# Linear attention's norm and gate as a stream of their own, and sample values that no longer wait for the mix

## The chip, the cores and the metric

The kernel runs on one core of a Trainium2 chip. The metric is the time of one execution on the device in microseconds. The kernel before took 2499.03 us (median of three runs, 2498.38 to 2510.2).

## The reference, cut to what matters

One layer of a hybrid decoder is computed for 1024 prompt tokens and for 32 sample tokens (8 sequences of 4), in fp32. After a first feed-forward network, one projection gives the columns of four mixers; their outputs go through `w_out`, and a second feed-forward network follows. Two mixers matter here.

The first is linear attention with a decaying state:

```
qe, ke, kd = q * exp(b), k * exp(-b), k * exp(b_last - b)      # b: running sum of the log decay in a chunk
att   = tril(qe @ ke.T);  o = att @ v + qe @ S                 # S: state of 32 x 64 per head, 4 heads
S     = exp(b_last) * S + kd.T @ v                             # from chunk to chunk
o     = o * rsqrt(mean(o * o) + EPS)  * norm_g * silu(g)       # per head: the norm and the gate
```

Prompt chunks have 64 tokens. The sample tokens are eight chunks of 4, each with a state of its own that is read from memory, and whose new state is an output.

The other is dilated attention: three groups of four heads with windows of 128, 512 and 2048 at dilations of 1, 4 and 16. The outputs of the three groups are merged with weights from their softmax denominators. The sample tokens attend to cached keys and values, 36 loads of 256 KB for the values alone.

## The kernel before, in words

**The mainline and the streams.** The large products form one sequence, `line()`, the mainline. Beside it run streams: Python generators that each issue a few instructions and yield. A recording layer, `Loom` (L1399), decides at build time in which order all of this is written down: it keeps a planned time for each engine, lets the stream with the best priority go that is ready (`run`, L1574), and takes the next step of the mainline (`weft`, L1530) where none is ready or where PE would be short of dense work. A stream can yield a condition (a lambda); it is then held until the condition is true. The engines work off their queues in the recorded order. On the chip itself nothing is decided.

**The stage of the change.** It begins behind the RWKV mixer and holds linear attention (`gla`), dilated attention (`dil`) and the last parts of the mainline: the remaining projection columns (products named `pw`, L139, L142, L143) and then the first half of the output projection (products named `pz`, L2897, 432 of them). When the mainline has reached its end, only the streams are left. The stage after it begins with the second half of the output projection (L204), which reads the mixers' results from the tiles `xl`.

**Linear attention** works in five pieces: four of 256 prompt tokens, and the 32 sample tokens. It has two streams of equal priority `GP` = 0.9. `operands` (L2422) loads q, k, v and the decays of a piece (tiles gq, gk, gv, gmn), makes `qe`, `ke`, `kd`, turns v and kd (products into `pm`, L2468 and L2485) and appends the operands to `made`; it is at most two pieces ahead. `outputs` (L2490) takes a piece, loads its gate columns into `ggt`, computes `o` (tile go) by `chunks` (L2507: L2514 state increments, L2530 scores, L2539 scores by values, L2543 query by state) or for the last piece by `sample` (L2553), and then norms and gates it by `gate` (L2594). In `sample` the products are L2561 (scores), L2573 (by values), L2576 (query by state, on the tile gSF, which POOL clears and ACT fills) and L2589 (the state's increments, from the tile gex). In `gate`, ACT squares `o` (L2600), PE takes the mean (L2606), DVE computes the reciprocal root in three steps (`rsqrt_steps`, L1009) and spreads it (L2610, tile gsp), PE turns it (L2616), DVE multiplies (L2618), POOL applies the gate (L2619), and two transfers write `mixd`. A piece's products begin only when the piece before it is gated: all of it is one generator.

**Dilated attention** has six heads' halves, which `prep` (L1998) loads and turns (kv: the sample rows, L2033), and 24 blocks of `attend` (L2054): scores L2065, softmax on DVE and ACT, turned weights L2096 copied to the tile pT (L2100 on ACT, L2102 on DVE, a ring of four), products with values L2107. `merge` (L2145) merges the groups in eight steps: two loads `ot` per step, DVE L2197 to L2202 and POOL L2199, then PE turns the result (L2206) into the tiles `mix`, which exist from the 20th block on. `sample` (L2211) first scores the cached keys (L2229; the window of 128 with products L2271 and L2276), then waits until `mix` exists, then runs `dil_sample` (L2282): 36 loads of values into a ring of four tiles (cv), 72 products (L2347), and at the end the result is turned (L2358) and copied into `mix`. `join` splits `mix` into `xl` by thirds of the tokens.

**What follows.** `mixes01` loads linear attention's result (mx from `mixd`) and splits it into `xl`, three thirds with two loads each. The first weights of the next stage are cast on ACT (L111) and on POOL (L112). The results of L204 go through DVE, ACT and POOL into the norm of the next stage and come back to PE as L312.

Of the kernel before, what the change touches and what calls it, by code (L numbers as in the profile page):

```python
# [11 lines left out]
F32 = mybir.dt.float32  # L12
F32R = mybir.dt.float32r
AF = mybir.ActivationFunctionType
# [6 lines left out]
TP = 1024  # L21
# [1927 lines left out]
def dil(L, pool, wload, xs3):  # L1949
# [48 lines left out]
    def prep(g, p, H):  # L1998
# [32 lines left out]
        nc.tensor.transpose(q[:32, 256:384], qs, ident)  # L2031
        kv = ap.tile([32, 3, 128], F32, name="kv", tag="kv", bufs=1)
        nc.scalar.copy(kv.rearrange("t u x -> t (u x)"), q[:32, 0:384])  # L2033
# [177 lines left out]
    def sample():  # L2211
        yield from dil_sample_keys(L, ap, qd, qz, caches, sT, groups, ps)
        yield lambda: len(mix) > 0
        yield from dil_sample(L, ap, tab[:, 384:], qz, kts, vs, caches, sT, mix, ps)
        sampled.append(1)
# [66 lines left out]
def dil_sample(L, ap, bias, qz, kts, vs, caches, sT, mix, ps):  # L2282
# [50 lines left out]
    for b0 in range(0, 8, 2):  # L2333
# [6 lines left out]
        for xs in ((0,), (1, 2), (3, 4), (5, 6), (7, 8)):  # L2340
# [11 lines left out]
            for i in range(len(xs)):  # L2352
                fetch(j - len(xs) + i + NR)
            yield 0.0
    q = ps("pa")
    for p in range(2):
# [22 lines left out]
def gla(L, ap, cold, mixd):  # L2379
# [19 lines left out]
    nc.vector.memset(scans.rearrange("p (c t) -> p c t", t=4)[:, :, 0:1], 0.0)  # L2399
    rows = ap.tile([3, 128], F32, name="glarows", tag="ga")  # L2400
    L.dma(rows[0:1], I["gla_b_alpha"])
# [9 lines left out]
    pieces = ((0, 256), (256, 256), (512, 256), (768, 256), (TP, TS))  # L2411
    made, through = [], [0]

    def tile(tag, shape=(128, 256), bufs=1):
        return ap.tile(list(shape), F32, name="g" + tag, tag="g" + tag, bufs=bufs)
# [6 lines left out]
    def operands():  # L2422
# [4 lines left out]
        yield lambda: L.loom.got(GLA)  # L2427
        al = [ap.tile([16, TH], F32, name="gal", tag=g) for g in ("ggt", "go", "gv")]
        for t in range(NTH):
# [60 lines left out]
    def outputs():  # L2490
        for j, (a, w) in enumerate(pieces):
            cl, nch, nt, n = dims(a, w)
            yield lambda: len(made) > j
            qe, ke, kn, Vn, ends = made[j]
            gt = tile("gt", (128, 2, 256))[:, :, :w]
            for p in range(2):
                L.dma(gt[:, p], cold["gla_g%d" % p][:, a:a + w])
            yield 0.0
            o = tile("o", (128, 2, 256))[:, :, :w]
            if a < TP:  # L2500
                yield from chunks(j, o, *made[j])
            else:
                yield from sample(o, *made[j])
            yield from gate(a, w, o, gt)
            through[0] = j + 1

# [87 lines left out]
    def gate(a, w, o, gt):  # L2594
# [3 lines left out]
        st = ap.tile([128, 8], F32, name="gst", tag="gst")[:n, :m]  # L2598
        sqs = tile("aT", (128, 2, 256))[:, :, :w]
        nc.scalar.activation(sqs, o, AF.Square)  # L2600
        yield
        q = ps("pt")
        for p in range(2):
            for i in range(nt):
                j = (p * nt + i) * 2
                nc.tensor.matmul(q[:n, j:j + 2], sqs[:, p, i * n:(i + 1) * n], b2m, start=True, stop=True)  # L2606
        nc.vector.tensor_scalar(st, q[:n, :m], EPS, None, op0=OP.add)
        rn = yield from rsqrt_steps(L, ap, st, (n, m), "grs")
        sp = ap.tile([128, 8, 64], F32, name="gsp", tag="gaT")[:n, :m]
        nc.vector.tensor_copy(sp, rn.unsqueeze(2).to_broadcast([n, m, 64]))  # L2610
        yield
        q = ps("pt")
        for p in range(2):
            for i in range(nt):
                j = (p * nt + i) * 2
                nc.tensor.transpose(q[:, p * w + i * n:p * w + i * n + n], sp[:, j:j + 2].rearrange("p h c -> p (h c)"), ident[:n, :n])  # L2616
        for p in range(2):
# [5 lines left out]

    return operands(), outputs()

# [554 lines left out]
```

## Time and profile before

| | |
|---|---|
| time, median of three runs | 2499.03 us |
| the profiled execution | 2503.86 us |
| its span, first to last instruction | 2502.1 us |
| mean granted clock of PE | 0.972 |

The span is that of one profiled execution, so sums are made against 2503.86 us. In the profile, PE is TensorE's matmuls, PEld its weight loads, DVE VectorE, ACT ScalarE, POOL GpSimd and SP the queue that issues most loads. A row of a group reads: line, engine, operation, output and inputs by the program's names, sizes, count, then busy us and mean ns of one, then the idle time of the engine just before them and what ended it. An fp32 product that the program records once shows as two rows in the trace (two passes); a turn (transpose) shows as one.

### The profile page before, as it was taken

The page shows a single profiled execution, that of the slowest core. Times are in us where ns is not written, and L with a number is a line of the kernel's source. Part 1 is how long each engine was busy: PE and PEld are TensorE (multiplying, and loading weights), DVE is VectorE, ACT ScalarE, POOL GpSimd, SP SyncE. Part 2 cuts the span into 40 slices and gives each one's busy share as a digit, 9 for nine tenths or more (in the row PEclk, how much of TensorE's full clock was granted, in tenths as well). Part 3 has the DMA queues.
Part 4 walks back from the last instruction along what each step waited for, and adds up shares of the span by engine and source line. Part 5 has one row for each costly group of instructions (what it writes and reads, how often), then busy time and mean ns, then how long its engine had stood idle before and what let it go on. Part 6 is the DMA issues. An engine that isn't in the chain of part 4 may idle for free. (4 is left out here: it accounts for less than half of the span.)

```text
span 2502.1 us, 41009 instructions
## 1 busy us (share of the span) xinstructions
PE 2411.0 (96%) x15543; PEld 2207.7 (88%) x15543; DVE 1395.5 (56%) x3211; ACT 1013.6 (41%) x2175; POOL 1067.8 (43%) x902
## 2 busy tenths in 40 slices
PE   8999999999999999999999999968999999999997
PEld 8999999977789998898888899737989999997777
DVE  7645454367775056665632467437854444447767
ACT  5433333366554242323324344415533333336651
POOL 3655555567643233232111111114355555557664
PEclk9999999999999999999989889969999999999999
DMA  4322222323434333231226676444222222233334
GB/s 133 100 69 83 66 82 68 106 86 111 119 126 132 93 106 90 87 100 52 74 56 195 185 228 184 134 130 146 79 86 74 80 74 80 72 103 92 104 103 148
DMA packets 273612, 265.21 MB, mean 106 GB/s; under 512 B 36283, under 2 KB 247380, under 8 KB 273414
## 3 DMA queue, kind: packets, MB, share of 16 engines
q1 hardware_dynamic: 223810, 212.69, 28.9%
q10 hardware_dynamic: 49604, 49.90, 5.8%
q8 instruction: 122, 2.00, 0.3%
q14 instruction: 76, 0.62, 0.1%
HBM read 195.26 MB, written 67.16 MB: 105 GB/s over the span
## 5 line engine op out<-in xcount | busy, mean ns | idle before, releaser
L520 POOL TENSOR_TENSOR wlo<-wraw,whi 128x512 fp32r<-128x512 f32 x280 | 379.7, 1374 | 355.1 <-ACT whi L519 355.0
L549 PE MATMUL p<-xh,whi 128*128 128x352 f32 x1120 | 364.0, 325 | 5.4 <-DVE hid L475 3.6
L551 PE MATMUL p<-xh,wlo 128*128 128x352 f32 x1120 | 362.3, 323 | 0.0
L550 PE MATMUL p<-xl,whi 128*128 128x352 f32 x1120 | 361.2, 322 | 0.0
L519 ACT CAST whi<-wraw 128x512 fp32r<-128x512 f32 x280 | 166.5, 620 | 409.1 <-PE p L550 293.4
L112 POOL TENSOR_TENSOR wlo<-wraw,whi 128x1024 fp32r<-128x1024 f32 x61 | 146.0, 2396 | 391.8 <-ACT whi L111 343.6
L139 PE MATMUL pw<-xh,whi 128*128 128x352 f32 x888 | 308.1, 347 | 2.3 <-ACT stg L2782 1.5
L143 PE MATMUL pw<-xh,wlo 128*128 128x352 f32 x888 | 293.4, 330 | 0.0
L142 PE MATMUL pw<-xl,whi 128*128 128x352 f32 x888 | 293.1, 330 | 0.0
L549 PEld LDWEIGHTS p<-xh,whi 128*128 128x128 f32 x1120 | 211.4, 189 | 6.8 <-DVE hid L475 3.9
L550 PEld LDWEIGHTS p<-xl,whi 128*128 128x128 f32 x1120 | 211.5, 189 | 0.0
L551 PEld LDWEIGHTS p<-xh,wlo 128*128 128x128 f32 x1120 | 210.4, 188 | 0.0
L139 PEld LDWEIGHTS pw<-xh,whi 128*128 128x128 f32 x888 | 171.5, 193 | 13.3 <-issue 7.5
L142 PEld LDWEIGHTS pw<-xl,whi 128*128 128x128 f32 x888 | 172.1, 194 | 1.9 <-issue 1.7
L143 PEld LDWEIGHTS pw<-xh,wlo 128*128 128x128 f32 x888 | 171.2, 193 | 1.4 <-issue 1.2
L549 PE MATMUL p<-hid,whi 128*128 128x352 f32 x400 | 129.9, 325 | 1.8 <-ACT n L583 1.4
L551 PE MATMUL p<-hid,wlo 128*128 128x352 f32 x400 | 129.8, 324 | 1.4 <-POOL wlo L520 1.4
L550 PE MATMUL p<-hid,whi 128*128 128x352 f32 x400 | 129.2, 323 | 0.0
L111 ACT CAST whi<-wraw 128x1024 fp32r<-128x1024 f32 x61 | 63.9, 1048 | 118.7 <-PE pw L142 85.2
L723 PE MATMUL p<-xh,hid 128*128 128x512 f32 x320 | 109.8, 397 | 0.1
L204 PE MATMUL pt<-whi,ya 128*128 128x256 f32 x512 | 97.7, 290 | 1.0 <-POOL ya L793 1.0
L839 DVE TENSOR_TENSOR y<-y,p 128x512 f32<-128x512 f32 x112 | 76.6, 685 | 38.7 <-PE p L723 36.7
(641 smaller groups left out, 5861.9 us busy)
## 6 DMA issues: line engine op xcount, KB each, us to landing
wraw<-in_w_ff_gate_dram SPq DMA_DIRECT2D x44, 512.0 KB
wraw<-in_w_ff_up_dram SPq DMA_DIRECT2D x44, 512.0 KB
wraw<-in_w_in_dram SPq DMA_DIRECT2D x37, 512.0 KB
wraw<-in_w_ff_down_dram SPq DMA_DIRECT2D x36, 512.0 KB
hid_d<-tmp ACTq DMA_DIRECT2D x60, 176.0 KB
hid_d<-n ACTq DMA_DIRECT2D x60, 176.0 KB
cv<-in_cache_win_dram SPq DMA_DIRECT2D x36, 256.0 KB
whi<-hid_d SPq DMA_DIRECT2D x32, 256.0 KB
```

What stands on the lines that cost most here:

```text
L112: nc.gpsimd.tensor_tensor(lo, raw, hi.bitcast(F32), op=OP.subtract)
L139: ins = nc.tensor.matmul(out, a, xh[:, cs], start=(first and i == 0), stop=False)
L142: nc.tensor.matmul(out, a, xl[:, cs], start=False, stop=False)
L143: nc.tensor.matmul(out, b, xh[:, cs], start=False, stop=(last and i == n - 1))
L204: nc.tensor.matmul(out, xs[kx][a][:, cs], ws[js[0]][b][:, kw], start=u == a == b == 0, stop=u == len(kk) - 1 and a == 1, skip_group_check= ...
L519: nc.scalar.copy(t[0][:, i], v)
L520: nc.gpsimd.tensor_tensor(t[1][:, i], v, t[0][:, i].bitcast(F32), op=OP.subtract)
L549: nc.tensor.matmul(out, ah, xh, start=first and k == 0, stop=False, skip_group_check=True)
L550: nc.tensor.matmul(out, ah, xl, start=False, stop=False, skip_group_check=True)
L551: nc.tensor.matmul(out, al, xh, start=False, stop=k == KH - 1, skip_group_check=True)
L723: nc.tensor.matmul(out, a[i][:, u], b[j][:, u], start=first and u == i == j == 0, stop=u == n - 1 and i == 1, skip_group_check=True)
L839: (nc.vector.tensor_copy if h else nc.scalar.copy)(v, p) if copy else nc.vector.tensor_add(v, v, p)
```

## The change

There are four parts. First, `gla` returns three streams: `gates` is new, between `operands` and `outputs`. `outputs` now only computes `o` and appends it to `raw`; `gates` loads the gate columns of a piece and norms and gates it, while `outputs` goes on with the next piece. For that `o` has two buffers (tag `go`). Second, the gate's squares and spreads are done in two halves of one tile `gsq`, in the place of the tiles gaT and gsp, which it shared with the scores. Third, the sample stream of dilated attention waits before its values for all six halves to be loaded and turned, and for `mix` only where it writes into it. Fourth, some tiles move: `kv` has no buffer of its own and takes one of the ring pT, and the first tiles of linear attention take other tags.

```diff
-        kv = ap.tile([32, 3, 128], F32, name="kv", tag="kv", bufs=1)
+        kv = ap.tile([32, 3, 128], F32, name="kv", tag="pT", bufs=4)
...
     def sample():
         yield from dil_sample_keys(L, ap, qd, qz, caches, sT, groups, ps)
-        yield lambda: len(mix) > 0
+        yield lambda: ready[0] == len(heads)
         yield from dil_sample(L, ap, tab[:, 384:], qz, kts, vs, caches, sT, mix, ps)
...
             yield 0.0
+    yield lambda: len(mix) > 0
     q = ps("pa")
     for p in range(2):
...
         for j, (a, w) in enumerate(pieces):
             cl, nch, nt, n = dims(a, w)
             yield lambda: len(made) > j
-            qe, ke, kn, Vn, ends = made[j]
+            o = tile("o", (128, 2, 256), 2)[:, :, :w]
+            if a < TP:
+                yield from chunks(j, o, *made[j])
+            else:
+                yield from sample(o, *made[j])
+            through[0] = j + 1
+            raw.append(o)
+
+    def gates():
+
+        for j, (a, w) in enumerate(pieces):
+            yield lambda: len(raw) > j
             gt = tile("gt", (128, 2, 256))[:, :, :w]
             for p in range(2):
                 L.dma(gt[:, p], cold["gla_g%d" % p][:, a:a + w])
             yield 0.0
-            o = tile("o", (128, 2, 256))[:, :, :w]
-            if a < TP:
-                yield from chunks(j, o, *made[j])
-            else:
-                yield from sample(o, *made[j])
-            yield from gate(a, w, o, gt)
-            through[0] = j + 1
+            yield from gate(a, w, raw[j], gt)
...
-        sqs = tile("aT", (128, 2, 256))[:, :, :w]
-        nc.scalar.activation(sqs, o, AF.Square)
-        yield
         q = ps("pt")
         for p in range(2):
+            sqs = tile("sq")[:, :w]
+            nc.scalar.activation(sqs, o[:, p], AF.Square)
             for i in range(nt):
...
-        sp = ap.tile([128, 8, 64], F32, name="gsp", tag="gaT")[:n, :m]
-        nc.vector.tensor_copy(sp, rn.unsqueeze(2).to_broadcast([n, m, 64]))
         yield
         q = ps("pt")
         for p in range(2):
+            sp = tile("sq")[:n, :128 * nt]
+            nc.vector.tensor_copy(sp.rearrange("n (h c) -> n h c", c=64),
+                                  rn[:, 2 * nt * p:2 * nt * p + 2 * nt].unsqueeze(2).to_broadcast([n, 2 * nt, 64]))
...
-    return operands(), outputs()
+    return operands(), gates(), outputs()
```

Because the order is written at build time, the change moves instructions of the whole stage. Three places show it. In the rows below, lines of the changed kernel are one to six higher than before where the diff stands above them: L2897 becomes L2902, L2358 becomes L2359, L2561, L2573, L2576 and L2589 become L2567, L2579, L2582 and L2595, and L2963 becomes L2968.

The first is PE where it turns the first cached keys of the window of 128 (c1k). Before, this stood there:

```order
L2096 MATMUL pm<-ident,s 128x128 x7
L2271 MATMUL pm<-ident,c1k 128x128 x4
L2897 MATMUL pz<-whi,xl 128x256
L2897 MATMUL pz<-wlo,xl 128x256
L2897 MATMUL pz<-whi,xl 128x256 x2
L2897 MATMUL pz<-wlo,xl 128x256
L2897 MATMUL pz<-whi,xl 128x256
L2616 MATMUL pm<-ident,gsp 128x128
L2271 MATMUL pm<-ident,c1k 128x128 x4
L2616 MATMUL pm<-ident,gsp 128x128 x3
L2107 MATMUL po<-Vn,pT 128x64 x4
```

Now linear attention's sample piece stands there (gq, gk, gSF), and dilated attention's scores (kT, qT):

```order
L2567 MATMUL pm<-gq,gk 32x32
L2065 MATMUL pm<-kT,qT 128x128 x8
L2271 MATMUL pm<-ident,c1k 128x128 x4
L2579 MATMUL pgo<-gaT,gVn 64x32 x2
L2582 MATMUL pgo<-gq,gSF 128x4 x8
L2902 MATMUL pz<-whi,xl 128x256
L2902 MATMUL pz<-wlo,xl 128x256
L2271 MATMUL pm<-ident,c1k 128x128 x4
L2065 MATMUL pm<-kT,qT 128x128 x14
L2276 MATMUL pm<-qz,kt_15913 128x8 x4
L2276 MATMUL pm<-qz,kt_15920 128x8 x4
L2902 MATMUL pz<-whi,xl 128x256
```

Ten rows further, with three more pz products between, the other seven L2582 follow, and then 22 pz products in a row. Fewer products of the mainline stand between the small steps here than before.

The second is PE at the end of the stage, up to the first L204. Before:

```order
L2347 MATMUL pm<-cv,Z 16x256 x3
L2576 MATMUL pgo<-gq,gSF 128x4 x8
L2347 MATMUL pm<-cv,Z 16x256 x8
L2358 MATMUL pm<-ident,A 128x128 x3
L2206 MATMUL pm<-ident,on 128x128 x2
L2606 MATMUL pm<-gb2m,gaT 32x2 x2
L2589 MATMUL pm<-gex,gkn 32x512 x4
L2206 MATMUL pm<-ident,on 128x128 x2
L2616 MATMUL pm<-ident,gsp 128x32 x2
L2206 MATMUL pm<-ident,on 128x128 x2
L204 MATMUL pt<-whi,xl 128x256
```

Now:

```order
L2347 MATMUL pm<-cv,Z 16x256 x5
L2206 MATMUL pm<-ident,on 128x128 x2
L2347 MATMUL pm<-cv,Z 16x256 x11
L2347 MATMUL pm<-cv,A 16x256 x2
L2206 MATMUL pm<-ident,on 128x128 x2
L2347 MATMUL pm<-cv,Z 16x256 x13
L2206 MATMUL pm<-ident,on 128x128 x2
L2347 MATMUL pm<-cv,Z 16x256 x3
L2359 MATMUL pm<-ident,A 128x128 x3
L2206 MATMUL pm<-ident,on 128x128 x2
L204 MATMUL pt<-whi,xl 128x256
```

Linear attention's rows (L2576, L2606, L2589, L2616) are gone from the end and stand before the last pz row; the sample values and the merges remain.

The third is SP's queue at the same end, where the last loads of the stage and the first of the next are issued. Before:

```order
L79 DMA cv<-in_cache_win_dram 128x2x256 x4
L79 DMA ot<-dil_o 128x2x128 x5
L79 DMA out_dram<-gVn 128x8x64
L79 DMA mix_d_88<-go 128x32
L79 DMA mix_d_89<-go 128x32
L79 DMA wraw<-in_w_ff_gate_dram 128x8x128
L2963 DMA mx<-mix_d_88 128x352
L2963 DMA mx<-mix_d_89 128x352
```

Now:

```order
L79 DMA ot<-dil_o 128x2x128
L79 DMA cv<-in_cache_win_dram 128x2x256 x4
L79 DMA ot<-dil_o 128x2x128
L2968 DMA mx<-mix_d_88 128x352
L2968 DMA mx<-mix_d_89 128x352
L79 DMA wraw<-in_w_ff_gate_dram 128x8x128
L2968 DMA mx<-mix_d_88 128x352
L2968 DMA mx<-mix_d_89 128x352
```

The writes of the new state (gVn) and of the last gated piece (go) have moved to an earlier place, among the cv loads.

More of the change, by code (lines that the diff above doesn't have):

```diff
@@ L2399, in gla @@
     nc.vector.memset(scans.rearrange("p (c t) -> p c t", t=4)[:, :, 0:1], 0.0)
-    rows = ap.tile([3, 128], F32, name="glarows", tag="ga")
+    rows = ap.tile([3, 128], F32, name="glarows", tag="ggt")
     L.dma(rows[0:1], I["gla_b_alpha"])
@@ L2411, in gla @@
     pieces = ((0, 256), (256, 256), (512, 256), (768, 256), (TP, TS))
-    made, through = [], [0]
+    made, raw, through = [], [], [0]
     def tile(tag, shape=(128, 256), bufs=1):
@@ L2427, in operands @@
         yield lambda: L.loom.got(GLA)
-        al = [ap.tile([16, TH], F32, name="gal", tag=g) for g in ("ggt", "go", "gv")]
+        al = [ap.tile([16, TH], F32, name="gal", tag=g, bufs=b) for g, b in (("ggt", 1), ("go", 2), ("go", 2))]
         for t in range(NTH):
@@ L2598, in gate @@
         st = ap.tile([128, 8], F32, name="gst", tag="gst")[:n, :m]
-        sqs = tile("aT", (128, 2, 256))[:, :, :w]
-        nc.scalar.activation(sqs, o, AF.Square)
+        q = ps("pt")
+        for p in range(2):
+            sqs = tile("sq")[:, :w]
+            nc.scalar.activation(sqs, o[:, p], AF.Square)
+            for i in range(nt):
+                j = (p * nt + i) * 2
+                nc.tensor.matmul(q[:n, j:j + 2], sqs[:, i * n:(i + 1) * n], b2m, start=True, stop=True)
+        nc.vector.tensor_scalar(st, q[:n, :m], EPS, None, op0=OP.add)
+        rn = yield from rsqrt_steps(L, ap, st, (n, m), "grs")
         yield
@@ L2603, in gate @@
         for p in range(2):
+            sp = tile("sq")[:n, :128 * nt]
+            nc.vector.tensor_copy(sp.rearrange("n (h c) -> n h c", c=64),
+                                  rn[:, 2 * nt * p:2 * nt * p + 2 * nt].unsqueeze(2).to_broadcast([n, 2 * nt, 64]))
             for i in range(nt):
[L2605 to L2608, printed above, removed]
-        sp = ap.tile([128, 8, 64], F32, name="gsp", tag="gaT")[:n, :m]
-        nc.vector.tensor_copy(sp, rn.unsqueeze(2).to_broadcast([n, m, 64]))
-        yield
[L2612 to L2616, printed above, removed]
+                nc.tensor.transpose(q[:, p * w + i * n:p * w + i * n + n], sp[:, i * 128:i * 128 + 128], ident[:n, :n])
         for p in range(2):
```

## The prediction

> **What bounds the kernel now.** First I read the page, whose first two parts say which engine carries the span.
>
> ```profile
> span 2502.1 us, 41009 instructions
> PE 2411.0 (96%) x15543; PEld 2207.7 (88%) x15543; DVE 1395.5 (56%) x3211; ACT 1013.6 (41%) x2175; POOL 1067.8 (43%) x902
> ...
> PE   8999999999999999999999999968999999999997
> ...
> PEclk9999999999999999999989889969999999999999
> ```
>
> PE is busy 96% of the span, so a microsecond that PE loses anywhere is a microsecond of the kernel. The digits show one slice where it loses much: PE at 6 and the granted clock at 6, slice 27 of 40, 1626 to 1689 us. That is the end of the stage that holds linear attention and dilated attention. Next I cut that stage by PE's own rows: from the third-piece products of linear attention (1411.86) to the last mainline product pz (1630.70), from there to the first L204 product of the next stage (1680.70), and the 90 us behind it. The columns are stretch, its length, then busy us per engine, the granted clock, the DMA share and GB/s.
>
> ```profile
> 1411.86:1630.70 218.84, 216.30 (x1721) 189.06 (x1721) 132.41 (x425) 96.87 (x292) 30.51 (x33) 0.95 0.61 187
> 1630.70:1680.70 50.00, 32.33 (x158) 14.24 (x157) 21.14 (x76) 9.45 (x26) 5.66 (x8) 0.65 0.41 122
> 1680.70:1770.00 89.30, 75.48 (x573) 70.44 (x572) 67.20 (x221) 47.95 (x120) 37.31 (x24) 0.91 0.45 143
> ```
>
> I call them front, tail and sequel. In the front PE idles 2.5 us of 219. In the tail it idles 17.7 of 50 and has a clock of 0.65: the mainline is used up, and only small steps are left. What they are is in PE's groups of the tail (count, busy, mean ns, idle before and its releaser).
>
> ```profile
> L2347 PE MATMUL pm<-cv,Z 128*16 128x256 f32 x72 | 16.3, 527 | 2.6 <-DMA cv<-in_cache_win_dram 2.5
> L2576 PE MATMUL pgo<-gq,gSF 128*128 128x4 f32 x32 | 5.5, 306 | 0.0
> L2589 PE MATMUL pm<-gex,gkn 32*32 32x512 f32 x8 | 3.8, 1056 | 3.2 <-DVE gex L2583 3.2
> L2573 PE MATMUL pgo<-gaT,gVn 32*64 32x32 f32 x8 | 1.0, 265 | 0.0
> L2561 PE MATMUL pm<-gq,gk 32*32 32x32 f32 x8 | 1.0, 202 | 2.4 <-ACT A L2351 2.0 <-DVE gaT L2562 0.3
> L2616 PE MATMUL pm<-ident,gsp 32*128 32x32 f32 x2 | 0.4, 286 | 2.5 <-DVE gsp L2610 2.5
> L2606 PE MATMUL pm<-gb2m,gaT 128*32 128x2 f32 x4 | 0.4, 198 | 1.3 <-ACT dmix L2207 1.3
> ```
>
> L2347 is dilated attention's sample values, fed by the cv loads. The other six lines are linear attention's sample piece, the fifth of five, and its gate. The end of the tail in order of time:
>
> ```profile
> 1662.04 0.90 PE L2358 MATMUL pm<-ident,A 128*128 128x128 f32 x3 [0.84 <-ACT A L2351]
> 1662.73 0.64 PE L2206 MATMUL pm<-ident,on 128*128 128x128 f32 x2
> 1664.70 0.37 PE L2606 MATMUL pm<-gb2m,gaT 128*32 128x2 f32 x4 [1.33 <-ACT dmix L2207]
> ...
> 1670.11 1.92 PE L2589 MATMUL pm<-gex,gkn 32*32 32x512 f32 x4 [3.19 <-DVE gex L2583]
> 1676.09 0.69 PE L2206 MATMUL pm<-ident,on 128*128 128x128 f32 x2 [4.07 <-DVE rst L1017]
> 1679.27 0.39 PE L2616 MATMUL pm<-ident,gsp 32*128 32x32 f32 x2 [2.49 <-DVE gsp L2610]
> 1680.35 0.69 PE L2206 MATMUL pm<-ident,on 128*128 128x128 f32 x2 [0.68 <-DVE go L2618]
> ```
>
> The sample values are done at 1662.9; the 18 us after that belong to linear attention's last state update and gate, with the last two merges (L2206) drawn out between them, since DVE works both off in order.
>
> **The change part by part.** The recorded order decides most of it. In the new order linear attention's sample piece and its gate stand whole before the last pz row; the tail holds sample values and merges alone. The sample values do not move: they begin 360 pz products into the 432 before and 366 now, although they no longer wait for the mix.
>
> *The tail shrinks.* At the last pz row 28 of the 72 L2347 products are recorded, against 32 before. So 14 of the 36 cv tiles are used, and with a ring of four 18 tiles are still to be issued, with nine ot loads between them: 18 x 0.262 MB + 9 x 0.131 MB = 5.9 MB. The rate is that of the first of these stretches, where linear attention hardly intervened yet:
>
> ```profile
> 1632.00:1648.00 16.00, 11.21 (x63) 4.13 (x63) 4.64 (x24) 2.15 (x7) 0.61 (x1) 0.89 0.76 234
> ...
> 1648.00:1662.00 14.00, 13.20 (x64) 7.29 (x64) 4.09 (x9) 2.95 (x8) 2.55 (x3) 0.54 0.44 130
> 1662.00:1680.70 18.70, 6.90 (x24) 2.51 (x24) 12.16 (x42) 3.14 (x10) 2.49 (x4) 0.50 0.06 14
> ```
>
> 5.9 MB at 234 GB/s take 25.2 us. To that I add the closing steps by the rows above: 0.84 and 0.90 for L2358, and for the last merge, which DVE reaches behind a mix load, as much as L2206 waited at worst, 4.1. That makes 31 us in the place of 50.0: **-19**. The bounds are 27 us, with the merge wholly hidden (-23), and 41, if half of the bytes come at the 130 GB/s that was left of the rate after 1648 (12.6 + 22.7 + 5.8; -9).
>
> *The front grows.* The six lines now run under the mainline, where PE has no room to spare. L2576 has a warm and a cold half:
>
> ```profile
> 1647.26 1.97 PE L2576 MATMUL pgo<-gq,gSF 128*128 128x4 f32 x16
> 1654.09 3.58 PE L2576 MATMUL pgo<-gq,gSF 128*128 128x4 f32 x16
> ```
>
> Twice 1.97 is 3.9; L2589 ran after 1662, at a clock of 0.50, so 1.9 of its 3.8; the others 1.0 + 1.0 + 0.4 + 0.4. That is 8.6, less the six products that leave the front for the tail: twelve passes at 0.23 (16.3 / 72), partly cold, 2.6 or a little less. **+6**; the bounds are +5, with the short ones halved too, and +13, if half of the idle time before these lines in the tail (9.4) comes along uncovered and the six products save nothing.
>
> *The clock in the front.* This is where the order speaks against the change. The clock of PE fell in the front while PE had no idle time at all:
>
> ```profile
> 1425.00:1430.00 5.00, 5.00 (x36) 4.79 (x35) 2.88 (x10) 1.16 (x3) 0.00 (x0) 1.00 0.80 242
> 1430.00:1440.00 10.00, 10.00 (x44) 8.57 (x44) 5.47 (x32) 1.94 (x7) 0.00 (x0) 0.66 0.77 229
> 1455.00:1475.00 20.00, 20.00 (x99) 17.75 (x99) 11.13 (x28) 5.83 (x19) 1.88 (x3) 0.66 0.70 214
> ...
> 1427.45 3.18 PE L2065 MATMUL pm<-kT,qT 64*128 64x128 f32 x20
> ```
>
> What stood there was a row of thin products, 64 of 128 array rows, without mainline between; the 20 took 3.18 us, and behind them the clock halved. The new order makes a longer row: L2065 eight times and fourteen times (44 passes, 44 x 0.159 = 7.0 us), both halves of L2576 (3.9) and eight L2276 with as few columns (16 passes by L2576's 0.123: 2.0), with five mainline products in all of it. All of it is thin, as was the row at 1427, and at 12.9 us it is four times as long. That row is the nearest, so I take the clock to be down after the first 3.2 us: 9.7 us of work at half speed, 9.7 lost. The bounds are 0 and 12.9. Against it stands what may go: 1455 to 1475 lost 20 x 0.34 = 6.8 us, and the steps of that place stand otherwise now; I take less than half, 3 (bounds 0 and 6.8). **+7** (-7 to +13).
>
> The Trainium skill, "TensorE: Matmul & The Clock Gate", section "What's actually happening", has the clock fall after an idle window of about 3.4 us. By that rule the new row, in which PE idles nowhere, would lose nothing. This trace does not agree: 0.66 granted in 1430 to 1440 with 10.00 of 10.00 us busy.
>
> *The sequel.* The last mix loads of linear attention were issued after the tail, and the next weights wait behind them in SP's queue:
>
> ```profile
> SPq L2963 <- DMA mx<-mix_d: 2.8, 1, 2.8
> ...
> PE ptx L312 <- ACT hn L304: 9.5, 3, 5.8
> PE pt L204 <- POOL wlo L112: 2.5, 2, 1.3
> PE pt L204 <- ACT whi L111: 0.5, 1, 0.5
> ```
>
> In the new SP order two of those four loads stand right behind the last ot load, with no write of the gate ahead of them, and POOL's line to the weights is free of the last gate. The 3.0 us of L204's waits for weights should go. The 9.5 us of L312 I leave: its chain starts sooner, but the new order also places the first L312 23 L204 rows earlier. **-3** (-9 if a good half of L312's wait goes too, +3 if the earlier row waits for the old chain).
>
> *At nothing.* Squares and spreads of the gate come in two halves, one more ACT and one more DVE instruction for each of five pieces.
>
> ```profile
> L2600 ACT ACTIVATE gaT<-go x5: 256/630/632, 1417.0 to 1657.9; 128x512 f32<-128x512 f32 x4, 128x64 f32<-128x64 f32 x1
> ```
>
> None can cost more than a whole square again, 0.63; uncovered that is 5 x 2 x 0.63 = 6 us, but in the front ACT is busy 97 of 219 us and DVE 132. The kv copy shares the ring pT, so five later pT copies on DVE or ACT wait for its three writes; behind them in line stand the softmax steps of the next block, and PE's products for them. The writes are issued a block or more ahead, which covers them; uncovered, each could cost what SP waited for one mix transfer, 2.8, five times 14. Writes of the sample piece now stand in SP's queue among cv loads, but DVE makes them ready before PE frees the cv buffer that the next load wants.
>
> Sum: -19 + 6 + 7 - 3 = **-9 us**. The profiled execution took 2503.86 (span 2502.1 and 1.8 around it), 4.8 above the median of the three runs; -9 gives 2494.9 there, and on the median 2499.03 it gives **2490**.
>
> **The rivals.** A difference under 0.5% (12.5 us) is about what a measurement of this kernel can't tell from none.
>
> *The clock holds.* If the new row of thin products is broken up enough by the five mainline products and its transposes, +10 falls away: -19, 2480. For it: the 100 us from 1500 on, the last blocks of dilated attention with many thin steps, at a clock of 1.00. Against it: 1430 to 1440, and that the mainline was dealt out more evenly there.
>
> ```profile
> 1500.00:1600.00 100.00, 97.68 (x918) 89.13 (x918) 68.68 (x216) 49.92 (x154) 14.47 (x15) 1.00 0.54 164
> ...
> L2271 PE MATMUL pm<-ident,c1k x16: 272/273/303, 1569.9 to 1582.7; 128*128 128x128 f32 x16
> ```
>  By the rule of the Trainium skill ("TensorE: Matmul & The Clock Gate", above) this would be the outcome.
>
> *The tail stays long.* The change would then not do what it says. The sample values are bound by loads and start no earlier, and if the merges between them, now five of them in PE's line, each hold PE back until DVE is through, the tail is 41 us: -9 + 6 + 7 - 3 = +1, 2500. For it: the 4.07 us that one such step idled PE at 1676. Against it: the DVE rows behind those waits were linear attention's.
>
> *The clock does not come back.* The end on the other side. Behind the thin row stand 171 of the 432 pz products, mixed with thin steps; if few stretches of them are dense enough, the half clock lasts towards the last pz; the front has some 60 us of work left there (the L2271 in whose neighbourhood the row stands began at 1569.9 before, and the front ended at 1630.7). Low all the way, 60 us of work at half speed lose 60; low for half of the way they lose 30, in place of the +7: -9 - 7 + 30 = +14, 2513. It decides from 9 + 12.5 = 21.5 us of further loss on. For it: 1455 to 1475 stayed low for most of 20 us. Against it: 22 pz products stand right behind the row, and in all cases of the front the clock came back.
>
> **How the numbers follow.** Forecast 0.52, of which 0.08 lies beyond -12.5; clock holds 0.28; tail long 0.12; clock stays down 0.08. Faster by over 0.5%: 0.28 + 0.08 = 0.36; within: 0.44 + 0.12 = 0.56; slower: 0.08. The range takes the forecast's terms at about half of their bounds, the clock rival and the long tail, and leaves out its ends and most of the last rival: 2474 to 2507.
>
> **What would show it.** Right: the stretch from the last pz to the first L204 is 27 to 35 us, with no linear attention in it; the front is longer by 10 to 16 us, with a new dip of the granted clock where L2065 stands with L2582 (the old L2576); L204's waits for weights are gone. Wrong: a tail above 40; PE idle in the front above 8 us, with waits for gSF, gex or pT; a clock of 1.00 through that row; or a total beyond the range.

## The result and the profile after

The changed kernel took 2513.47 us (median of 8 runs, 2506.13 to 2528.75), the kernel before beside it 2498.7 us (8 runs, 2493.21 to 2510.2): ratio 1.0063, 95% interval 1.0035 to 1.0091. It is slower by 15 us. The forecast was 2490, the range 2474 to 2507. The profiled execution took 2511.46 us. First the page's engines and digits:

```profile
span 2509.7 us, 41009 instructions
PE 2421.8 (96%) x15543; PEld 2216.6 (88%) x15543; DVE 1399.6 (56%) x3216; ACT 1013.9 (40%) x2180; POOL 1069.0 (43%) x902
...
PE   8999999999999999999999999988999999999997
...
PEclk9999999999999999999999879899999999999998
```

The deep hole of slice 27 is gone from both rows. Ahead of it, in slices 23 to 26, which hold the front, the granted clock reads 8, 7, 9, 8, where it read 8, 8, 9, 9 before. I cut both kernels at the same instructions: the front from the first query product of linear attention on its state (L2543 before, L2549 after; the written order is the same up to there) to the last pz, the tail to the first L204, then 90 us of sequel. Front and tail of before, and the stretch of its 61st to 120th pz:

```profile
1400.43:1630.75 230.32, 227.78 (x1787) 200.22 (x1787) 134.27 (x429) 100.97 (x307) 31.70 (x36) 0.93 0.59 180
1630.75:1680.69 49.94, 32.27 (x158) 14.18 (x157) 21.12 (x76) 9.45 (x26) 5.64 (x8) 0.65 0.41 122
1504.38:1520.53 16.15, 16.15 (x144) 15.48 (x142) 12.01 (x36) 6.64 (x20) 1.29 (x1) 1.00 0.81 253
```

and the changed kernel, front, tail, sequel and three places in the front (length, busy us of PE, PEld, DVE, ACT, POOL, granted clock, DMA share, GB/s):

```profile
1393.92:1660.04 266.12, 256.71 (x1837) 220.43 (x1837) 144.20 (x459) 103.65 (x317) 35.83 (x39) 0.88 0.51 155
1660.04:1693.92 33.88, 21.68 (x108) 6.70 (x107) 16.54 (x55) 8.27 (x23) 5.72 (x6) 0.85 0.72 220
1693.92:1783.22 89.30, 77.05 (x600) 73.35 (x600) 70.30 (x244) 49.73 (x125) 34.91 (x22) 0.92 0.39 136
1487.40:1533.40 46.00, 42.37 (x252) 34.95 (x251) 26.73 (x89) 12.98 (x44) 3.96 (x7) 0.74 0.46 141
1585.60:1609.80 24.20, 24.12 (x198) 22.72 (x197) 7.55 (x31) 13.95 (x42) 4.82 (x3) 0.86 0.32 97
...
1492.70:1516.60 23.90, 23.90 (x97) 19.52 (x96) 12.00 (x46) 6.51 (x25) 1.18 (x3) 0.50 0.33 101
```

The tail is 16.1 us shorter. The front is 35.8 longer, and the rows split that: PE idle (length less busy) 9.4 in place of 2.5, +6.9; lost to the clock (length times one minus the clock) 31.9 in place of 16.1, +15.8; the rest, work at full clock, +13.1. (The clock is printed with two digits, which leaves about 1 us open: by the clock's own records the front has 64.6 us at half clock in place of 30.2, so 32.3 lost in place of 15.1.) From the first L204 to the first L549 product on `hid`, just behind the place from which the written order is the same again, it is 140.7 in place of 143.7, -3.0. Ahead of the front, where nothing was changed, this execution was 6.5 us faster by chance, and 2.7 faster behind that product; so the two spans differ by 7.5, the medians by 15, and front, tail and sequel by 16.7.

A single execution says little of a loss that varies. The mean granted clock of every run is on record, and gives the loss of the whole span: 68 us in the mean of the eight runs of the changed kernel (62 to 75 with two standard errors), 58 to 61 in the three batches of the kernel before that ran beside the experiments. So about 8 of the 15 us are lost to the clock over the whole program, and the other half is work and idle time. The front alone loses more than that, but the tail gives 12.4 us of it back: 17.5 (49.94 at 0.65) before, 5.1 (33.88 at 0.85) now.

The fourth row of the changed kernel's cuts is the worst place. It holds the 61st to the 120th pz: 46.0 us, where before they took 16.15 at a clock of 1.00 (third row above). PE in order of time there:

```profile
1488.02 0.28 PE L2902 MATMUL pz<-whi,xl 128*128 128x256 f32 x1
1490.50 1.29 PE L2065 MATMUL pm<-kT,qT 64*128 64x128 f32 x4 [2.20 <-DVE gSS L2525]
...
1495.04 1.30 PE L2065 MATMUL pm<-kT,qT 64*128 64x128 f32 x4
...
1496.27 1.97 PE L2107 MATMUL po<-Vn,pT 128*128 128x64 f32 x8
1498.17 1.30 PE L2065 MATMUL pm<-kT,qT 64*128 64x128 f32 x4
1499.40 1.22 PE L2536 MATMUL pm<-gq,gk 32*128 32x128 f32 x4
...
1507.87 1.97 PE L2549 MATMUL pgo<-gq,gSS 128*128 128x64 f32 x8
1509.77 1.77 PE L2065 MATMUL pm<-kT,qT 64*128 64x128 f32 x10
```

PE waits 2.2 us for DVE. Then scores of dilated attention (L2065) and a whole piece of linear attention (L2536, L2549) come together, with small groups of mainline products between them. From 1492.7 to 1516.6 the granted clock is 0.50 while PE is busy 23.90 of 23.90 us (the last row of the cuts). The wait comes from DVE's order: two splits of an earlier mixer's result, fed by loads, stood ahead of the state updates that free the product tile.

```profile
1483.72 3.13 DVE L129 TENSOR_TENSOR xl<-mx,xl 128x352 fp32r<-128x352 f32 x2
1486.78 3.67 DVE L2525 SCALAR_TENSOR_TENSOR gSS<-gSS,gends,pm 32x64 f32<-32x64 f32 x12
1490.48 1.21 DVE L2525 SCALAR_TENSOR_TENSOR gSl<-gSS,gends,pm 32x64 f32<-32x64 f32 x4
```

### The profile page after: what moved, and what is told of

Read it like the earlier page. It is cut to its first block, busy times and chain, and to the rows that moved or that the text cites. A ratio compares the mean times of both kernels' runs of the same rounds, so it can differ in the third digit from the quotient of the medians.

```text
span 2509.7 us, 41009 instructions
## 1 busy us (share of the span) xinstructions
PE 2421.8 (96%) x15543; PEld 2216.6 (88%) x15543; DVE 1399.6 (56%) x3216; ACT 1013.9 (40%) x2180; POOL 1069.0 (43%) x902
## 5 line engine op out<-in xcount | busy, mean ns | idle before, releaser
L549 PE MATMUL p<-xh,whi 128*128 128x352 f32 x1120 | 364.7, 326 | 4.3 <-DVE hid L475 3.5
L112 POOL TENSOR_TENSOR wlo<-wraw,whi 128x1024 fp32r<-128x1024 f32 x61 | 146.5, 2402 | 401.8 <-ACT whi L111 357.6
L549 PEld LDWEIGHTS p<-xh,whi 128*128 128x128 f32 x1120 | 211.8, 189 | 5.8 <-DVE hid L475 3.8
L549 PE MATMUL p<-hid,whi 128*128 128x352 f32 x400 | 130.1, 325 | 2.0 <-ACT n L583 1.8
L204 PE MATMUL pt<-whi,ya 128*128 128x256 f32 x512 | 98.3, 291 | 1.1 <-POOL ya L793 1.1
```

Source lines behind the costliest of these rows:

```text
L112: nc.gpsimd.tensor_tensor(lo, raw, hi.bitcast(F32), op=OP.subtract)
L204: nc.tensor.matmul(out, xs[kx][a][:, cs], ws[js[0]][b][:, kw], start=u == a == b == 0, stop=u == len(kk) - 1 and a == 1, skip_group_check= ...
L549: nc.tensor.matmul(out, ah, xh, start=first and k == 0, stop=False, skip_group_check=True)
```

## The experiments

Theory 1: the new order puts thin steps closer together, and the clock of PE follows the density of its work. Theory 2: the time is what the change adds (a stream with its waits, halves, shared buffers). In all kernels below "the stage" is the stretch from linear attention's first instruction to the last pz, 64 to 69 us more than the front (78 and 84 in the two kernels with added products). In the table, lost is length times one minus the clock, and work is what is left without lost and idle. The columns up to the tail come from one profiled execution each; the next one is the span times one minus the recorded clock, over all runs, uncertain by 2 to 7 us (two standard errors). The ratio is to runs of the kernel before on the same chip beside it (medians 2495.4 to 2499.4), with its 95% interval.

| kernel | stage | clock | lost | idle | work | tail | lost, whole span, mean of all runs | median | ratio |
|---|---|---|---|---|---|---|---|---|---|
| before | 297.5 | 0.93 | 21 | 6 | 271 | 49.9 | 58 to 61 | 2498.7 | |
| changed | 332.5 | 0.89 | 37 | 12 | 284 | 33.9 | 68 | 2513.5 | 1.0063 (1.0035 to 1.0091) |
| one stream | 327.3 | 0.91 | 29 | 13 | 284 | 36.3 | 62 | 2512.9 | 1.0048 (1.0028 to 1.0068) |
| halves only | 328.0 | 0.89 | 36 | 9 | 283 | 35.9 | 62 | 2507.5 | 1.0051 (1.0032 to 1.0071) |
| one yield | 311.2 | 0.92 | 25 | 11 | 275 | 42.9 | 49 | 2494.4 | 0.9985 (0.9969 to 1.0002) |
| dense rows | 362.8 | 0.90 | 36 | 7 | 320 | 31.9 | 63 | 2541.7 | 1.016 (1.0137 to 1.0182) |
| narrow rows | 401.8 | 0.79 | 84 | 5 | 313 | 31.5 | 121 | 2594.1 | 1.0363 (1.0339 to 1.0386) |
| priorities 1 | 337.9 | 0.86 | 47 | 10 | 281 | 33.2 | 71 | 2518.3 | 1.0062 (1.0038 to 1.0086) |
| priorities 2, even | 315.2 | 0.91 | 28 | 8 | 279 | 34.7 | 46 | 2485.5 | 0.9951 (0.9934 to 0.9969) |
| priorities 3 | 343.9 | 0.89 | 38 | 11 | 295 | 17.7 | 63 | 2509.0 | 1.0031 (1.0013 to 1.005) |
| one yield, late | 339.7 | 0.91 | 31 | 9 | 300 | 17.8 | 57 | 2503.8 | 1.0027 (1.0012 to 1.0041) |
| before, even | 308.0 | 0.94 | 18 | 10 | 279 | 40.2 | 61 | 2502.0 | 1.002 (0.9998 to 1.0041) |
| one stream, even | 337.7 | 0.92 | 27 | 15 | 295 | 13.5 | 54 | 2499.2 | 1.0012 (0.9993 to 1.0031) |

**One stream.** The split undone, all else kept:

```diff
+            gt = tile("gt", (128, 2, 256))[:, :, :w]
+            for p in range(2):
+                L.dma(gt[:, p], cold["gla_g%d" % p][:, a:a + w])
+            yield 0.0
...
+            yield from gate(a, w, o, gt)
             through[0] = j + 1
-            raw.append(o)
...
-    return operands(), gates(), outputs()
+    return operands(), outputs()
```

> Everything of the change but the split: outputs gates its own piece again, all else (halves of the gate, buffers, the sample values' wait) as in the changed kernel. In the written order the sample piece of linear attention still leaves the tail (its 16 query products stand 300 to 354 pz into the 432), and the five pieces again stand early in the front. Theory 1 (the front is longer because its thin steps stand closer together and the clock of PE falls): the front has about 60 us at half clock as in the changed kernel (64.6), the tail is 32 to 38 us, the whole 2505 to 2515. Theory 2 (the new stream itself costs the time, by waits that it adds): the cold time of the front goes back to about 30 us, the short tail stays, the whole is 2485 to 2500.

2512.9: the loss stays without the new stream. Theory 2 in this form falls. The half-clock time of its front was 46 us, below the 60 expected, and over all its runs it loses 62 us to the clock where the kernel before beside it loses 61: its warmer tail balances its front, and its 13 us are work and idle time.

**Halves only.** The kernel before with the gate's halves alone (the diff's part on `gsq`), kv in the ring pT, and one small tile (`glarows`) under another tag.

> The kernel before with one thing of the change alone: the gate's squares and spreads in halves of a tile of their own (and kv in the ring pT, which makes the room for it). The written order of PE, DVE, ACT and POOL is then word for word that of the one-stream kernel, which measured 2512.9. If the order is what decides: 2508 to 2518. If the second buffer of o, the later wait of the sample values or the earlier load of the gate columns had a part in the loss: nearer to 2499.

2507.5, just under the range, and a ratio of 1.0051 like the 1.0048 of the one-stream kernel. So of the four parts, this one, with a tile of its own for the squares and one yield fewer, turned the order; under the old priorities the stream, the second buffer of `o` and the new wait of the sample values add nothing that shows. That wait was not run alone, but the one-stream kernel has the new one and the halves-only kernel the old one, and all rows of PE, DVE, ACT and POOL stand in the same order in both traces.

**One yield.** In the kernel before:

```diff
         nc.scalar.activation(sqs, o, AF.Square)
-        yield
```

> The kernel before with a single yield taken out, the one behind the gate's square. Not one instruction is added, removed or resized, but the planner writes another order: linear attention's query products stand 0 to 312 pz into the mainline instead of 0 to 360, the sample piece's begin at 396 instead of behind the last pz. Theory 1: the order alone makes the front colder (half-clock time 40 to 60 us, against 30 before), the tail gets a little shorter (42 to 48 us, since the last state updates are still in it), the whole is 2500 to 2512. Theory 2 (the time came from what the change adds: a stream, halves, shared buffers): no change, 2496 to 2502.

2494.4: below what Theory 1 gave, and by the ratio no different from before, as Theory 2 had it. Theory 1's signs were right (4 us more lost in the stage, tail 7 shorter), their sum was not: it left out that the tail is warmer (0.95 in place of 0.65), so that over the whole span this kernel loses 49 us, 12 less than the kernel before beside it. A shuffled order is not slow in itself.

**Dense rows and narrow rows.** Products added ahead of the scores (`attend`), which the planner passes over; the second kernel has `ident[:32], tab[:32, 0:128]` in their place and differs in nothing else:

```diff
+                if h == 0:
+                    nc.tensor.matmul(Q[h][:, u * 256 + x * 128:u * 256 + x * 128 + 128], ident, tab[:, 0:128],
+                                     start=True, stop=True)
+                    L.loom.unseen.add(L.loom.ins[-1].name)
```

> The changed kernel with 70 products added in its score steps, each 128 rows by 128 columns in fp32, on a bank that the score product behind it overwrites; the planner does not see them. They do nothing but make the thin stretches denser, and by 2 x 0.11 us each they take some 15 us of PE. Theory 1 (density sets the clock): the half-clock time of the front falls from 64.6 us to some 35, which gives back 15 us, and the whole is 2507 to 2517, the added work coming nearly free. Theory 2 (the loss is in waits and in more work, and the clock follows something else): half-clock time stays at 55 to 75 us and the whole is about 2513 + 15 = 2529.

> The same as the kernel with 70 added products of 128 rows, word for word in the same order, but each added product has 32 rows in place of 128; its time in PE at full clock is the same. Theory 1 (density sets the clock): half-clock time in the front of some 105 us, 35 us more in the whole than with 128 rows: 2540 to 2555. Theory 2: no difference between the two kernels, about 2529 both.

Stage of the kernel with 128 rows, and of the one with 32:

```profile
1326.40:1689.15 362.75, 355.95 (x2370) 298.87 (x2371) 162.85 (x566) 142.28 (x414) 47.82 (x46) 0.90 0.50 155
```

```profile
1334.11:1735.88 401.77, 397.25 (x2370) 329.69 (x2371) 160.71 (x566) 142.48 (x414) 47.34 (x46) 0.79 0.46 140
```

The pair shows what lowers the clock here. The order is the same word for word and so is the number of products; with 32 rows the stage loses 48 us more to the clock (0.21 of 401.77 against 0.10 of 362.75), and the medians differ by 52. Theory 2 gave no difference. PE is idle *less* in the colder kernel, 4.5 against 6.8 us, so idle time is not what lowers the clock here. The Trainium skill, "TensorE: Matmul & The Clock Gate", section "What's actually happening", has the clock fall after an idle window; this pair does not agree. By themselves both came out above Theory 1, by 25 and 39 us, and the gain that it forecast for the wide rows did not come: 36 us are lost in the stage where the changed kernel loses 37, and the front has 51 us of half-clock time where 35 were forecast (131 with 32 rows, where some 105 were). I also priced an added product at 0.22 us, and the work column says 0.5 (320 - 284 = 36 us for 70). Counted in the trace from each row's start to the next one's, with time at half clock counted half, the added products take 27 us, 0.2 a pass in place of 0.11, and the score products beside them 11 us more than in the changed kernel. Why they take longer was not tried.

**Three other orders of the changed kernel.** Only priorities were moved, no instruction:

```
                   GP   SPR  OPR  MPR
changed kernel     0.9  0.8  1.0  1.1
priorities 1       1.0  0.9  1.1  1.1
priorities 2       1.2  0.9  1.1  1.0
priorities 3       1.0  0.9  0.9  1.1
```

> The changed kernel with three of the planner's priorities moved (linear attention 0.9 to 1.0, sample values 0.8 to 0.9, dilated attention's loads 1.0 to 1.1); no instruction is added, removed or resized, only the order is another. Theory 1 (density sets the clock) makes a count from the written order: each PE row with the duration that it has at full clock, its columns times the share of its 128 array rows summed per window of 3.41 us, clock halved behind a window under 2000 and back behind one over 2500, mean over 16 phases of the window. (It gives for the fronts run so far 12, 32, 23 and 18 us lost to the clock, where half of the measured half-clock time is 15, 32, 23 and 20: before, changed, one stream, one yield.) From the stage's first row on it gives 33 us lost here and 26 in the changed kernel, with 1 us less work and a tail of 35 us: 7 us slower than the changed kernel, 2520 (2512 to 2528). Theory 2 (the time is what the change adds, and the tail): 2513, no difference from the changed kernel.

2518.3, but a ratio of 1.0062 beside the changed kernel's 1.0063: this does not tell the theories apart. In the profile 47 us are lost, 10 more than in the changed kernel where 7 were counted.

> The changed kernel with other priorities (linear attention 1.2, sample values 0.9, loads of dilated attention 1.1, merge 1.0). No instruction is added, removed or resized. The written tail is as in the changed kernel, or two steps longer (52 value products behind the last pz, 46 there). Theory 1's count: 8.5 us lost to the clock from the stage's first row on, against 26, 1 us less work, tail 36 us: 16 us faster than the changed kernel, 2497 (2489 to 2505), with half-clock time in the front below 30 us. Theory 2: 2515, since tail and added parts are those of the changed kernel.

2485.5, 0.9951 (0.9934 to 0.9969): better than both kernels, 28 us under the changed one with the same instructions and nearly the same tail. Theory 2 gave 2515 and falls; Theory 1 gave 2497, so it had the direction and too small a gain. Its stage and tail, in its slowest run (2499.45), which is the one that was profiled:

```profile
1334.83:1650.01 315.18, 307.13 (x2222) 269.44 (x2223) 167.91 (x594) 142.19 (x417) 50.03 (x49) 0.91 0.58 178
1650.01:1684.66 34.65, 23.10 (x114) 6.88 (x115) 10.68 (x26) 7.21 (x18) 4.12 (x3) 0.85 0.69 214
```

Against the changed kernel even this run loses 8 us less to the clock, idles 3.6 less and has 6 less work at full clock. Over all its runs it loses 46 us to the clock where the changed kernel loses 68, so 22 of the 28 us are the clock's.

> The changed kernel with priorities 1.0 (linear attention), 0.9 (sample values), 0.9 (loads of dilated attention), 1.1 (merge). No instruction is added, removed or resized. The sample values begin 300 pz into the 432 in place of 366, and only 26 of their products stand behind the last pz. Theory 1's count: 14 us lost to the clock against 26, 7 us more work in the front, a tail of some 25 us in place of 34: 13 us faster than the changed kernel, 2500 (2492 to 2508). Theory 2: only work moved from the tail to the front, 7 - 9 = -2, 2511.

2509.0: the count missed, and Theory 2's 2511 is the nearer. In the profile its stage lost 38 us to the clock, as much as the changed kernel's.

**One yield, late.** The kernel of the single yield with GP 1.3, SPR 0.9, OPR 0.9, MPR 1.0.

> The kernel before without the yield behind the gate's square, and with priorities 1.3 (linear attention), 0.9 (sample values), 0.9 (loads of dilated attention), 1.0 (merge). No instruction is added, removed or resized. The sample values begin 306 pz into the 432; linear attention is whole before the last pz, without a stream of its own for the gate and without shared buffers; 22 value products are left for the tail. Theory 1's count: 4 us lost to the clock from the stage's first row on against 9 before, 16 us more work in the front, a tail of about 23 us in place of 50: 16 us faster than before, 2483 (2474 to 2492). Theory 2 (tail and moved work alone): 16 - 27 = -11, 2488.

2503.8, above both. The tail came as counted (17.8), but work in the stage rose by 29 us where 16 were counted. Its front has nearly the clock of before, 0.93 (41 us at half clock, 30 before):

```profile
1394.73:1669.86 275.13, 268.24 (x1917) 225.22 (x1917) 146.38 (x490) 106.81 (x322) 38.45 (x43) 0.93 0.55 166
```

but products that both kernels have took longer in it. Two groups of the late kernel:

```profile
L2896 PE MATMUL pz<-whi,xl 128*128 128x256 f32 x256 | 59.2, 308 | 1.1 <-ACT z L2910 1.1
L2065 PE MATMUL pm<-kT,qT 64*128 64x128 f32 x224 | 37.9, 363 | 0.2
```

and of the kernel before:

```profile
L2897 PE MATMUL pz<-whi,xl 128*128 128x256 f32 x256 | 53.7, 293 | 0.0
L2065 PE MATMUL pm<-kT,qT 64*128 64x128 f32 x224 | 31.4, 359 | 0.2
```

12 us more for the same 480 rows. The timeline shows a small part of it, at pz:

```profile
1644.18 0.59 PE L2347 MATMUL pm<-cv,Z 128*16 128x256 f32 x2
1644.71 0.39 PE L2896 MATMUL pz<-wlo,xl 128*128 128x256 f32 x1
1644.93 0.39 PE L2896 MATMUL pz<-whi,xl 128*128 128x256 f32 x2
1645.16 0.28 PE L2896 MATMUL pz<-wlo,xl 128*128 128x256 f32 x1
1645.28 0.28 PE L2896 MATMUL pz<-whi,xl 128*128 128x256 f32 x1
```

The pz behind a value product holds PE for 0.22 us (1644.71 to 1644.93), the next ones for 0.12 each (0.23 for two). Dealt out in small groups, the mainline pays that at each change of kind: over the whole front the first pz of a group holds PE for 0.22 us in the median (67 of them at full clock), the others for 0.12. But there are 69 such groups here and 46 in the front of before, and 23 x 0.10 is only 2.3 us. The scores rose more: counted from each row's start to the next one's, with time at half clock counted half, their 224 rows take 34.2 us here and 27.0 before, and what makes them longer was not tried.

**The even priorities without the change, and with one stream.**

> The kernel before, none of the change in it, with the four priorities of the even order (1.2, 0.9, 1.1, 1.0) that gave 2485 on the changed kernel. Theory A (these priorities are better by themselves): 2486, 13 us under the kernel before. Theory B (what counts is the one order that comes out, by its clock and its tail): the sample piece of linear attention still stands whole behind the last pz, the sample values begin 323 pz into the 432 and are mixed with the mainline, as in the two kernels that came out 9 and 20 us over the count. The count gives 7 us more than before (11 more lost to the clock, 4 more work, 8 less tail), and what those two went over it adds some 5: 2500 to 2514, most likely 2508.

> The changed kernel with outputs gating its own piece again (one stream), and the four priorities of the even order (1.2, 0.9, 1.1, 1.0). Theory A (priorities, whatever the streams): 2486. Theory B (the order that comes out): the sample values begin 306 pz into the 432, only 16 of them are left for the tail, and the front takes on all the rest; the count gives 2 us more than before, and the two kernels with such early sample values came out above the count: 2498 to 2512, most likely 2505. If B holds, the split into a stream of its own is worth some 20 us under these priorities, and nothing under the old ones.

2502.0 and 2499.2, both no different from before, both at the low end of Theory B. The 11 us more of lost time that B counted for the first did not come (18 us in the stage, 21 before). So the priorities are not better by themselves, and neither is the split. Together they are worth 0.5% against before; under these priorities the split brings 0.9951 in place of 1.0012.

## Why the prediction was wrong, by its own steps

The step that failed is the front. It was to grow by 13 us, 6 of work and 7 of clock, and grew by 35.8: 8.8 more of clock, 7.1 more of work, and 6.9 of idle time that had no term in the sum. Tail and sequel came within 3 us.

- **The tail shrinks, -19:** right. Measured -16.1, 33.9 us in place of 31, with no linear attention in it; 12.4 of the 16.1 are clock. What ends it is the last merge, as the sum had it:

```profile
1689.26 0.55 PE L2359 MATMUL pm<-ident,A 128*128 128x128 f32 x3 [0.83 <-ACT A L2351]
1693.75 0.41 PE L2206 MATMUL pm<-ident,on 128*128 128x128 f32 x2 [3.94 <-DVE on L2202]
```

- **The front grows, +6:** too small, +13.1 measured. Three of the four larger lines (below) took about what was priced or less. L2595 took 4.2 us where 1.9 were priced: I had halved its time in the tail, where the clock was at half. But there its rows began two at a time (6 ns apart), and a pair held PE for 0.85 us; in the front each row at full clock holds it for 0.45 or 0.52 alone. Counted from each row's start to the next one's, with time at half clock counted half, all rows of linear attention together take 13 us more in the front, where 8.6 were priced; the value products give back 1.1, where 2.6 were priced; and pz takes 2.3 more, which is the price of changing kind (67 groups of pz in place of 46).

```profile
L2595 PE MATMUL pm<-gex,gkn 32*32 32x512 f32 x8 | 4.2, 600 | 0.0
L2582 PE MATMUL pgo<-gq,gSF 128*128 128x4 f32 x32 | 4.0, 253 | 0.0
L2567 PE MATMUL pm<-gq,gk 32*32 32x32 f32 x8 | 1.0, 202 | 0.0
L2579 PE MATMUL pgo<-gaT,gVn 32*64 32x32 f32 x8 | 0.7, 264 | 0.0
```

- **The clock in the front, +7 (-7 to +13):** the largest of the three misses. "I take the clock to be down after the first 3.2 us: 9.7 us of work at half speed" was said of one row of thin products. That place (1585.60 to 1609.80) lost 3.4 us. The front as a whole lost 15.8 more than before, above my bound, and most of its loss came 70 to 150 us earlier, where scores and a piece of linear attention had come together. The kind of mechanism was right, and the pair of dense and narrow rows and the last section show it; I looked at the one place where the order looked worst and not at the whole front. The count that I made for the experiments gives 12 us for the front before and 32 for the changed one, but its two thresholds were fitted to these traces afterwards, and it missed later orders: priorities 3, one yield late, and the kernel before with the even priorities.
- **PE idle in the front, no term:** +6.9. The prediction named idle time above 8 us as a sign of being wrong; it is 9.4, in the waits for gSS, pT and others:

```profile
PE po L2107 <- ACT on L2110: 2.3, 1, 2.3
PE pm L2065 <- DVE gSS L2525: 2.2, 1, 2.2
PE po L2107 <- ACT pT L2100: 2.0, 1, 2.0
PE pm L2486 <- POOL gmn L2481: 1.9, 2, 1.4
PE pm L2621 <- DVE gsq L2618: 0.9, 1, 0.9
```

- **The sequel, -3:** right as far as it can be read. L204 waits for no weights any more, the 9.5 us of L312 became 10.8, and the stretch to the first L549 product on `hid` is 3.0 shorter; up to the end of the program it is 5.6.
- **At nothing:** nearly right as instructions: in the front PE waits 0.9 us for gsq, and 2.0 for one pT copy, which may or may not be kv's doing. What the halves do by themselves is to turn the written order; the sum had the new order before it, so this is not where it failed.
- **The rivals:** "the clock does not come back" gave 2513 with a chance of 0.08. The number is near, the mechanism was not that: from 1602 to the last pz no half clock is recorded.

What stays open: why the same products hold PE for longer in some orders (the added ones and the scores, above), and how the loss of each order could be counted before it runs.

## What to carry to other kernels

Where a planner writes the order, cost the order that comes out over the whole stage, not the edit: here the halves of one tile, which as instructions cost next to nothing, made the kernel 0.5% slower by themselves. Thin matmuls moved under a dense mainline are paid by their own time and by the clock, and a little by each change of kind, so a shorter tail is worth having only if the front stays dense. When an edit has turned the order, try a few neighbouring priorities before judging it: the same instructions ran in 2513 and in 2485 us.

## What the runs showed of the hardware

- The clock follows density, not idle time: 0.79 with PE idle 4.5 of 402 us, 0.90 with 6.8 of 363, in one and the same order.
- In all 13 traces the granted clock is either full or half, and it changes on a grid of 3.41 us alone. Take each window of that grid at full clock in the 13 fronts, and sum over the matmul rows that begin in it their columns times the share of the 128 array rows that they use. The sum tells what the clock does in the next window, and between 1500 and 2500 it leaves it open. Ahead of 41 of the 69 drops PE was busy for 99% of the window or more.

| sum in the window | windows | half clock in the next |
|---|---|---|
| under 1500 | 42 | 40 |
| 1500 to 2000 | 45 | 17 |
| 2000 to 2500 | 55 | 10 |
| 2500 to 3000 | 78 | 2 |
| 3000 and more | 574 | 0 |

- The same order meets the clock differently from run to run. The one-stream and the halves-only kernel have the same written order on PE, DVE, ACT and POOL, and their profiled stages show 0.91 and 0.89; in the unchanged stretch from 1290 to the front (below, before and changed) the same products took 110.4 us at 0.87 and 103.9 at 0.95. The same section of the Trainium skill calls the window free-running and the number of slow first products variable from run to run. These rows agree, and so does the grid: in the 13 traces it begins between 0.12 and 0.99 of a window behind the first instruction.

```profile
1290.00:1400.43 110.43, 107.26 (x643) 91.50 (x643) 33.16 (x144) 45.34 (x117) 17.41 (x12) 0.87 0.53 160
```

```profile
1290.00:1393.90 103.90, 100.73 (x644) 86.98 (x643) 34.25 (x144) 45.38 (x117) 17.74 (x12) 0.95 0.55 171
```

- A pz product directly behind one of another kind holds PE 0.22 us instead of 0.12 (L2347 ahead of L2896, above; medians of 0.20 to 0.22 and 0.12 in the fronts of before, the changed and the late kernel).
